# Two-layer encoder with mixture of experts: buffers placed ahead in 1 MB slots, and the latents' products behind the stick-breaking ones

## The chip, the cores and the metric

The kernel runs on one core of one Trainium2 chip. The metric is the time of one execution on the device, in microseconds (us); the time of a kernel is the median of its runs.

## The reference

Input x is 256 tokens by 1024 features, float32. Two layers, each with a mixer part and an expert part, then a last RMS norm. Cut to what matters:

```python
def hybrid_layer(x, ...):
    proj = rms_norm(x, norm1_g) @ w_in                   # 1024 -> 416 + 768 + 256
    ya = mla_mixer(proj[:, :256], proj[:, 256:384], proj[:, 384:416], ...)   # latents: 8 heads
    yb = stick_breaking_mixer(q, k, v)                   # 4 heads of 64, softplus and a reversed cumsum
    yc = pool_mixer(proj[..., o4:], pool_w, pool_scale)  # means over 2, 4, 8, 16 tokens
    x = x + concat(ya, yb, yc) @ w_out
    return x + hier_moe(rms_norm(x, norm2_g), ...)       # 4 groups x 8 experts of 256, top 2 of one group
def reference(x, ...):
    for l in range(2):
        x = hybrid_layer(x, ...)
    return rms_norm(x, final_g)
```

## The kernel before

All weights are float32 and are read once, in one ordered stream of tiles of 128 partitions by 16 KB (2 MB), each with one DMA from the queue of SP. The stream of a layer: the input projection in `a0` and `a1` (1.9 MB each), `v` (the columns of the stick-breaking values and of the pooling), `mid` (up-projections of the latents, pooling, router), `w0` and `w1` (output projection), 32 tiles `h00` to `h73` (gate and up weights of experts, 4 to each of 8 groups), and 16 tiles `d00` to `d33` (down weights: quarter of the features, pair of groups). The next layer's `a0`, `v`, `a1` stand among the `d` tiles, and `fg`, the gain of the last norm, behind `d13` of layer 1. `h22` is the third tile of group 2.

Memory for this stream and for large working buffers (`mHL`, the mixers' outputs in two parts; `wHL`, the split weights; `xHL`, the split input; `kq`, keys and queries; `tp`, transposed tokens and parts for the experts; `sHL`, stick-breaking weights in two parts) is given out by `Ring` (L49 to L115): 11 buffers of 2 MB (`pair`) and 3 of 1 MB (`one`), each taken from a list of free ones (`idle`) and given back as a whole. The program is built twice. The first build, the rehearsal, counts a tick at each take, get and drop of a buffer; `rehearsed` (L100) then gives each tile of the stream the first tick from which, up to its use, fewer than 11 pairs are taken. The second build issues the tile's DMA at this tick. It is a count only: which buffer a tile gets is decided by who is first in the list.

A layer in order of the program: `arrive` and `measure` transpose and square one quarter of the features at a time while the previous layer's expert quarters are added; `project_in(q, part)` (L343) multiplies quarter q with the input projection, parts 0 and 1 the 416 latent columns (12 products), parts 2 and 3 the 512 columns of the stick-breaking queries and keys (24 products). Every product of float32 weights is made of three, from a high and a low part of each operand, which DVE, ACT and POOL split off (`parts`, L224; `split` L256 goes 3 pieces ahead). In the last quarter each part has a step behind it: `scales` (L335, products of the inverse norms), `latents` (L382, square sums of the latents, and `dg`, the identity times the inverse norm), `rescale` (L398, latents times their norm), `heads` (L413, the product `ones` by `dg` that spreads the norms, and the scaled queries and keys).

`mixers` (L428) then does one value block, transposes the latents (L273), another value block, the stick-breaking scores (16 products, `zb`), and from there fills PE with what is left: in layer 0 six value blocks, then `keys(0)`, `keys(1)`, `latent_values`, four `latent_queries`; in layer 1, where six blocks of the values were done beside the experts, the keys, values and queries themselves. Between these stand the softplus pieces of ACT, for two heads each (Abs, Exp, Ln; L523 to L525), with a maximum and an addition on DVE (L530) and `stick_parts` (L504). Attention, the output projection and `route` follow; then `experts` (L836): `hidden(g)` takes 4 `h` tiles, `down` a half of a `d` tile. A buffer is given back when its last column is used. The program order of each engine is the order of the code; semaphores order the engines among one another.

Of the kernel before, what the change touches and what calls it, by code (L numbers as in the profile page):

```python
# [22 lines left out]
NPAIR, NONE = 11, 3  # L23
# [3 lines left out]
SM_UK, SM_UV, SM_PW, SM_RT = 2048, 2560, 3072, 3328  # L27
# [14 lines left out]
class Ring:  # L42
# [5 lines left out]

    def __init__(self, nc, pool, plan):  # L49
        self.nc, self.pool, self.plan = nc, pool, plan  # L50
        self.idle = {2: deque(range(NPAIR)), 1: deque(range(NONE))}
        self.stream, self.issued, self.now, self.cut = [], 0, 0, {}
        self.live, self.first, self.spans, self.kind = {}, {}, {}, {}

    def tile(self, dtype, n):
        i = self.idle[n].popleft()
        name = f"{('one', 'pair')[n - 1]}{i}"
        return n, i, self.pool.tile([128, 2048 * n], dtype, name=name, tag=name)

    def tick(self):  # L60
        self.now += 1
        while self.plan and self.issued < len(self.stream) and self.plan[self.issued] <= self.now:
            name, src, then = self.stream[self.issued]
            self.live[name] = self.tile(F32, 2)
            for a, b in self.cut.get(name, ((0, src.shape[1]),)):
                self.part(name, src, a, b)
            self.issued += 1
            for f in then:
                f()

    def part(self, name, src, a, b):

        self.nc.sync.dma_start(self.live[name][2][:src.shape[0], a:b], src[:, a:b])  # L73

    def take(self, name, dtype=F32, n=1):
        if self.plan:
            self.live[name] = self.tile(dtype, n)
        self.tick()
        self.first[name], self.kind[name] = self.now, n
        return self.live[name][2] if self.plan else self.pool  # L80
# [6 lines left out]
    def get(self, name):  # L87
        self.tick()
        self.first.setdefault(name, self.now)
        return self.live[name][2] if self.plan else self.pool  # L90

    def drop(self, *names):
        for n in names:
            if self.plan:
                size, i, _ = self.live.pop(n)
                self.idle[size].append(i)
            self.spans.setdefault(n, []).append((self.first.pop(n), self.now + 1))
        self.tick()

    def rehearsed(self):  # L100

        used = {n: np.zeros(self.now + 3, int) for n in (1, 2)}
        for name, v in self.spans.items():
            for a, b in v:
                used[self.kind.get(name, 2)][a:b] += 1
        assert used[1].max() <= NONE and used[2].max() <= NPAIR, (used[1].max(), used[2].max())
        plan, now, used = [], 1, used[2]
        for name, _, _ in self.stream:
            use = self.spans[name][0][0]
            full = np.flatnonzero(used[now:use] >= NPAIR)  # L110
            now = min(use, now + full[-1] + 1) if len(full) else now
            used[now:use] += 1
            plan.append(now)
        return plan
# [6 lines left out]
class Net:  # L121
    def __init__(self, tc, ctx, a, plan):
# [17 lines left out]
        def add(name, src, *then):  # L140
            r.stream.append((name, src, then))

        def w(l, *names, then=()):
            for n in names:
                add(f"{n}.{l}", a[n][l], *then)
# [3 lines left out]
        r.cut = {"a0.0": ((0, 928),), f"d33.{L - 1}": ((0, 2048), (2048, 3072), (3072, 4096))}  # L149
        rest = [lambda c=c: r.part(*r.stream[0][0:2], *c) for c in ((928, 1856), (1856, 3712))]  # L150
        w(0, "a0", then=[rest[0], load_x(1), rest[1], load_x(2), load_x(3)])
        w(0, "a1", then=[self.tables])
        w(0, "v")
        for l in range(L):
            w(l, "mid", "w0", "w1")
            for g in range(8):
                for i in range(4):
                    add(f"h{g}{i}.{l}", a["wh"][(l * 8 + g) * 4 + i])
            for q in range(4):
                for p in range(4):  # L160
                    add(f"d{q}{p}.{l}", a["wd"][(l * 4 + q) * 4 + p])
                if l + 1 < L:
                    w(l + 1, *(("a0", "v"), (), ("a1",), ())[q])
                elif q == 1:
                    add("fg", a["fg"])
# [67 lines left out]
    def weights(self, l):  # L233

        add = lambda name, c, n, last, how=0: self.feed.append((f"{name}.{l}", c, n, last, how))
        value = lambda k: add("v", k * 512, 512, k == 7)
        for q in range(4):
            for c, n in ((0, 416), (416, 512)):
                for k in (2 * q, 2 * q + 1):
                    add(f"a{k // 4}", k % 4 * 928 + c, n, c and k % 4 == 3, l + q == 0)  # L240
# [5 lines left out]
        add("mid", SM_UK, 512, False, 1)  # L246
        add("mid", SM_UV, 512, False, 1)
        for j in range(4):
            add("mid", j * 512, 512, False, 1)
        for c in (6, 7, 4, 5, 0, 1, 2, 3):  # L250
            for n in range(2):
                add(f"w{c < 4:d}", c % 4 * 1024 + n * 512, 512, n and c in (5, 3))
# [3 lines left out]
    def split(self, ahead=AHEAD):  # L256

        while self.feed and len(self.ready) <= ahead:
            name, c, n, last, how = self.feed.popleft()
            piece = self.ring.get(name)[:, c:c + n]  # L260
# [4 lines left out]
            if last:  # L265
                self.ring.drop(name)
# [68 lines left out]
    def scales(self):  # L335
# [5 lines left out]
        V.tensor_tensor(self.rr, self.rr, self.widths[:, None, :].to_broadcast([128, 2, 2]), op=OP.mult)  # L341

    def project_in(self, q, part):  # L343
# [3 lines left out]
        if part < 2:  # L347
# [6 lines left out]
        if q == 3:  # L354
# [765 lines left out]
```

## Time and profile before

| | us |
|---|---|
| runs | 631.49, 627.99, 627.11 |
| median | 627.99 |
| profiled execution | 630.48 |
| its span | 628.9 |
| PE busy | 539.5 (86% of the span) |
| DVE busy | 255.0 (41%) |
| ACT busy | 145.5 (23%) |
| POOL busy | 94.0 (15%) |
| stream of weights | 227.32 MB, 86.9% of the DMA engines' time |

The profile is of one execution. Busy time is a union of instructions; what matters for the end is where an engine is idle and what ended the idle time. 1.6 us of the profiled execution lie outside the span.

### The profile page before, as it was taken

How to read it: one execution, taken by the hardware profiler on the slowest of the kernel's cores; microseconds unless marked ns; L12 is line 12 of the kernel's file. 1: busy time of each engine (PE TensorE's matmuls, PEld its weight loads, DVE VectorE, ACT ScalarE, POOL GpSimd, SP SyncE). 2: the span in 40 equal slices, each digit the busy share in tenths (PEclk: the TensorE clock that was granted, in tenths of full speed). 3: DMA queues.
4: the chain of work that ended last, by engine and by line, in shares of the span. 5: the costliest groups of instructions: out<-in, count | busy, mean ns of one | idle time of the engine just before them, and what ended most of it. 6: DMA issues, size and time to landing. Idle time of an engine off the chain costs nothing. (4 is left out here: it accounts for less than half of the span.)

```text
span 628.9 us, 10437 instructions
## 1 busy us (share of the span) xinstructions
PE 539.5 (86%) x4296; PEld 360.4 (57%) x4296; DVE 255.0 (41%) x660; ACT 145.5 (23%) x359; POOL 94.0 (15%) x138
## 2 busy tenths in 40 slices
PE   8989999888888849699997899997888885849994
PEld 7959877454544415466666777753455551535662
DVE  4778665322232212423337776543322221111332
ACT  4466453100000011222224654410000001102221
POOL 2544222100000000111112232310000000000001
PEclk9999999989998888799999889999989988778998
DMA  8995667899999999999999156589999999999931
GB/s 319 417 422 244 267 269 287 350 399 426 428 426 430 423 425 425 428 429 422 431 427 425 68 209 271 214 348 430 428 428 426 426 428 426 424 427 426 425 153 68
DMA packets 18444, 228.69 MB, mean 364 GB/s; under 512 B 2129, under 2 KB 3409, under 8 KB 4690
## 3 DMA queue, kind: packets, MB, share of 16 engines
q1 hardware_dynamic: 17954, 227.32, 86.9%
q8 instruction: 37, 0.61, 0.4%
q10 hardware_dynamic: 432, 0.59, 0.3%
q14 instruction: 21, 0.17, 0.1%
HBM read 226.85 MB, written 1.05 MB: 362 GB/s over the span
## 5 line engine op out<-in xcount | busy, mean ns | idle before, releaser
L211 PE MATMUL ps<-pair,one 128*32 128x256 f32 (+2 forms) x2060 | 190.9, 502 | 19.9 <-PEq L966 13.4
L211 PE MATMUL ps<-pair,pair 128*128 128x512 f32 (+2 forms) x576 | 126.3, 365 | 4.0 <-POOL pair L229 2.3
L211 PEld LDWEIGHTS ps<-pair,one 128*32 128x32 f32 (+1 forms) x2060 | 62.4, 113 | 113.6 <-issue 87.8
L211 PEld LDWEIGHTS ps<-pair,pair 128*128 128x128 f32 x576 | 93.9, 192 | 28.7 <-issue 10.1
L211 PE MATMUL ps<-one,x 128*128 128x128 f32 x512 | 78.5, 317 | 29.1 <-DVE one L819 28.7
L211 PEld LDWEIGHTS ps<-one,x 128*128 128x128 f32 x512 | 72.1, 225 | 35.9 <-DVE one L819 35.7
L229 DVE TENSOR_TENSOR pair<-ps,pair 128x256 fp32r<-128x256 f32 (+1 forms) x74 | 31.9, 431 | 119.9 <-ACT pair L279 119.9
L229 POOL TENSOR_TENSOR pair<-pair,pair 128x512 fp32r<-128x512 f32 (+1 forms) x38 | 49.4, 1300 | 172.2 <-DVE pair L281 111.6
L279 ACT ACTIVATE pair<-ps 128x256 fp32r<-128x256 f32 (+2 forms) x80 | 33.1, 414 | 137.0 <-PE ps L211 136.6
L211 PE MATMUL ps<-pair 128*128 128x256 f32 (+1 forms) x320 | 61.3, 314 | 1.5 <-DVE low L560 0.6
L211 PEld LDWEIGHTS ps<-pair 128*128 128x128 f32 x320 | 46.0, 193 | 20.7 <-issue 15.8
L229 DVE TENSOR_TENSOR pair<-pair,pair 128x512 fp32r<-128x512 f32 (+1 forms) x54 | 46.6, 866 | 23.9 <-ACT pair L279 23.2
L868 ACT ACTIVATE one<-ps 128x256 f32<-128x256 f32 x16 | 6.1, 383 | 213.7 <-PE ps L211 213.7
L871 DVE TENSOR_REDUCE ws<-ps 128x1 f32<-128x256 f32 x16 | 6.8, 425 | 104.0 <-PE ps L273 104.0
L830 DVE TENSOR_TENSOR one<-ps,vec 128x512 f32<-128x512 f32 x32 | 22.1, 692 | 57.0 <-PE ps L211 56.8
L846 POOL TENSOR_TENSOR one<-one,comb 128x128 f32<-128x128 f32 x32 | 12.6, 399 | 192.3 <-DVE one L819 167.7
L279 ACT ACTIVATE pair<-pair 128x512 fp32r<-128x512 f32 (+1 forms) x54 | 32.7, 612 | 19.1 <-PE ps L211 9.3
L211 PE MATMUL ps<-ident,ones 128*128 128x128 f32 x172 | 28.7, 297 | 1.6 <-POOL ident L180 1.6
L273 PE MATMUL ps<-ident,one 128*128 128x128 f32 x128 | 23.3, 286 | 5.0 <-DVE pair L873 2.9
L273 PEld LDWEIGHTS ps<-ident,one 128*128 128x128 f32 x128 | 14.4, 141 | 22.3 <-issue 13.8
L211 PEld LDWEIGHTS ps<-ident,ones 128*128 128x128 f32 x172 | 24.2, 205 | 4.4 <-issue 2.8
L211 PE MATMUL ps<-one,pair 128*128 128x256 f32 x128 | 20.2, 314 | 4.5 <-DVE one L231 2.5
(138 smaller groups left out, 397.5 us busy)
## 6 DMA issues: line engine op xcount, KB each, us to landing
pair<-in_wh SPq DMA_DIRECT2D x64, 2048.0 KB, 18.8
pair<-in_wd SPq DMA_DIRECT2D x31, 2048.0 KB, 34.4
pair<-in_w SPq DMA_DIRECT2D x4, 2048.0 KB, 20.9
pair<-in_a SPq DMA_DIRECT2D x3, 1856.0 KB, 25.1
pair<-in_v SPq DMA_DIRECT2D x2, 2048.0 KB, 25.9
pair<-in_mid SPq DMA_DIRECT2D x2, 1808.0 KB, 20.6
x<-in_x SPq DMA_DIRECT2D x4, 256.0 KB, 5.8
pair<-in_wd SPq DMA_DIRECT2D x1, 1024.0 KB
```

The costliest lines, as they stand in the source:

```text
L211: self.nc.tensor.matmul(out, lhsT, rhs, start=start, stop=stop, skip_group_check=True)
L229: V.tensor_tensor(lo, in_, hi.bitcast(F32), op=OP.subtract)
L273: self.nc.tensor.transpose(out, in_, self.ident)
L279: nc.scalar.activation(out, in_, AF.Copy, scale=1.0 if scale is None else scale)
L830: self.nc.vector.tensor_tensor(xs[:, 4 * n:4 * n + 4], v3(self.ps[:, b0 + n], 4, 128), self.vec[:, l, 8 + 4 * n:12 + 4 * n, None].to_broad ...
L846: G.tensor_tensor(d4, d4, comb[:, t, 4 * g:4 * g + 4, None].to_broadcast([128, 4, 32]), op=OP.mult)
L868: A.activation(h, ps[:, 2, 0:256], AF.Silu)
L871: V.tensor_reduce(ws, ps[:, 3, 256:512], axis=AX.X, op=OP.add)
```

## The change

Memory stays 25 MB, now as 25 slots of 1 MB (`PAIRS = 12` pairs and a single one). All places are decided after the rehearsal: the working buffers first, each at a fixed place over its whole life, then the stream, tile after tile, in the places that are left. A tile has two halves (units) of 1 MB, which are got and dropped one by one. It is loaded with one DMA if a pair of slots is free, inside the experts ("calm") or if that is no later than the first half alone; otherwise with two DMAs, each half in a slot of its own. `a0` and `a1` are always loaded in halves. `fg` takes one slot. Column orders of `mid` and `w0` follow the halves. The core of `rehearsed`:

```diff
-        used = {n: np.zeros(self.now + 3, int) for n in (1, 2)}
...
-        plan, now, used = [], 1, used[2]
-        for name, _, _ in self.stream:
-            use = self.spans[name][0][0]
-            full = np.flatnonzero(used[now:use] >= NPAIR)
-            now = min(use, now + full[-1] + 1) if len(full) else now
...
+        for w in sorted(range(len(places)), key=lambda w: (-self.works[w][1], self.works[w][2] == F32, w)):
+            name, size, dtype, a, b = self.works[w]
...
+            busy[fit[0]:fit[0] + size, a:b] = True
...
+            first = alone(0, now)
+            if merge and len(units) == 2:
...
+                t, i = min((when((i, i + 1), now, ends), i) for i in range(0, n - 1, 2))
...
+                if t <= spans[0][0] and (t <= first[0] or calm[t]):
+                    plan.append((t, e, (0, 1), i))
```

In the last quarter the two products change places, with the steps behind them:

```diff
-            for c, n in ((0, 416), (416, 512)):
+            for c, n in ((416, 512), (0, 416)) if q == 3 else ((0, 416), (416, 512)):
...
-        if part < 2:
+        if (part < 2) != (q == 3):
...
-        if q == 3:
-            (self.scales, self.latents, self.rescale, self.heads)[part]()
+        if q == 3 and part != 2:
+            (self.scales, self.heads, None, self.latents)[part]()
```

`dg` is made in `scales`. `rescale` is called in `mixers`, all its evictions on DVE. There the scores `zb` come first, and one order serves both layers (`more(n)` does up to n value blocks, `soft(h, i)` is piece i of the softplus of heads h and h + 1):

```diff
+        soft(0, 0)
+        more()
+        soft(0, 1)
+        self.rescale()
+        soft(0, 2)
+        more()
+        soft(2, 0)
...
+        soft(0, 3)
+        self.parts(*ck, ps[:, 5, 0:256], vec[:, l, 18:19])
+        more(2)
+        soft(2, 1)
+        soft(2, 2)
         queries()
+        ring.drop("cw")
+        more(2)
+        soft(2, 3)
         ev("a", kv[64:128, 0::2], ps[64:128, 5, None, 256:512].to_broadcast([64, 4, 256]))
         ev("v", kv[0:64, 1::2], ps[0:64, 5, None, 256:512].to_broadcast([64, 4, 256]))
...
+        more(2)
+        ring.drop("xHL")
...
+        values_out()
+        stick_parts(0)
+        keys(0)
+        keys(1)
+        stick_parts(2)
+        latent_values()
```

On SP, in the mixers and the routing of layer 0, this is the order of the stream's transfers before: `h03`, `h10` to `h13`, `h20` to `h23`, each in a new buffer.

```order
L73 DMA pair_218<-in_wh 128x4096
L73 DMA pair_662<-in_wh 128x4096
L73 DMA pair_692<-in_wh 128x4096
L73 DMA pair_761<-in_wh 128x4096
L73 DMA pair_828<-in_wh 128x4096
L73 DMA pair_897<-in_wh 128x4096
L73 DMA pair_968<-in_wh 128x4096
L73 DMA pair_970<-in_wh 128x4096
L73 DMA pair_1081<-in_wh 128x4096
```

And now: `h03` (first row) to `h23` (last row), where `pair_116`, `pair_118` and `pair_120` are the places in which `h00`, `h01` and `h02` lie.

```order
L79 DMA pair_108<-in_wh 128x2048 x2
L79 DMA pair_110<-in_wh 128x2048 x2
L79 DMA pair_112<-in_wh 128x2048
L79 DMA pair_102<-in_wh 128x2048
L79 DMA pair_112<-in_wh 128x2048
L79 DMA pair_97<-in_wh 128x2048 x2
L79 DMA pair_114<-in_wh 128x2048
L79 DMA pair_102<-in_wh 128x2048
L79 DMA pair_114<-in_wh 128x2048
L79 DMA pair_964<-in_wh 128x4096
L79 DMA pair_116<-in_wh 128x4096
L79 DMA pair_118<-in_wh 128x4096
```

`h03` to `h20` now go out in halves, `h21` whole (`pair_964`), and `h22` goes into the place of `h00`, `h23` into that of `h01`.

On PE, from the last quarter of layer 1 on, before: the 12 latent products, the 24 of queries and keys, `ones`, a value block, the transposes, the other block, and the first scores.

```order
L211 MATMUL ps<-pair_2227,pair_2225 128x416 x12
L211 MATMUL ps<-pair_2225,pair_2227 128x256 x24
L211 MATMUL ps<-one_2226,ones 128x128 x2
L211 MATMUL ps<-pair_2227,pair_2225 128x512 x6
L273 MATMUL ps<-ident,one_2226 128x128 x8
L211 MATMUL ps<-pair_2227,pair_2225 128x512 x6
L211 MATMUL ps<-one_2900 128x256 x2
L211 MATMUL ps<-one_2900 128x128 x2
```

And now, from the 24 products to the keys (`one,pair_2177`, 256 columns):

```order
L280 MATMUL ps<-pair_2176,pair_2177 128x256 x24
L280 MATMUL ps<-pair_102,ones 128x128 x2
L280 MATMUL ps<-pair_2177,pair_2176 128x416 x12
L280 MATMUL ps<-one 128x256 x2
L280 MATMUL ps<-one 128x128 x2
L280 MATMUL ps<-one 128x256 x2
L280 MATMUL ps<-one 128x128 x2
L280 MATMUL ps<-pair_2177,pair_2176 128x512 x12
L343 MATMUL ps<-ident,pair_102 128x128 x8
L280 MATMUL ps<-one,pair_2177 128x256 x12
```

The latent products follow `ones`, the scores and both value blocks come before the transposes, and the keys right behind these.

On ACT at the same place before: the scaled norms, splits, the evictions of latent keys and queries (`ps,vec`), and the first Abs (L523) and Exp (L524) behind them.

```order
L421 ACTIVATE one_2900<-ps 128x256 x2
L279 ACTIVATE pair_2227<-pair_2559 128x512 x2
L279 ACTIVATE one_2939<-ps,vec 128x256 x3
L279 ACTIVATE pair_2940<-ps 64x4x256
L279 ACTIVATE one_2905<-ps,r_2816 128x512
L279 ACTIVATE pair_2227<-pair_2559 128x512
L279 ACTIVATE pair_2940<-ps 64x2x256
L523 ACTIVATE one_2938<-ps 128x768
L279 ACTIVATE pair_2940<-ps 64x2x256
L524 ACTIVATE one_2938<-one_2938 128x768
```

And now, from the first Abs (L529) on, with Exp (L531), Ln (L533) and the copy of `stick_parts` (L585):

```order
L529 ACTIVATE pair_108<-ps 128x768
L349 ACTIVATE pair_2177<-pair_118 128x512
L531 ACTIVATE pair_108<-pair_108 128x768
L533 ACTIVATE pair_108<-pair_108 128x768
L349 ACTIVATE pair_2177<-pair_118 128x512
L529 ACTIVATE pair_108<-ps 128x768
L349 ACTIVATE one<-ps,vec 128x256
L531 ACTIVATE pair_108<-pair_108 128x768
L533 ACTIVATE pair_108<-pair_108 128x768
L349 ACTIVATE one<-ps,vec 128x256 x2
L349 ACTIVATE pair_97<-ps 64x4x256
L349 ACTIVATE pair_102<-ps,r_2755 128x512
L585 ACTIVATE pair_141<-pair_108 128x768
```

The Exp and Ln of the second pair of heads now stand between the eviction of the latent keys and the two of the queries.

## Rows read from the trace of the kernel before

**Rows 1.** Page, part 2: GB/s in each of the 40 slices (15.7 us each).
```profile
GB/s 319 417 422 244 267 269 287 350 399 426 428 426 430 423 425 425 428 429 422 431 427 425 68 209 271 214 348 430 428 428 426 426 428 426 424 427 426 425 153 68
```

**Rows 2.** List of PE's waits: engine, line, releaser: us in total, times, longest.
```profile
PE ps L211 <- DMA pair<-in_fg: 7.9, 1, 7.9
...
PE ps L211 <- DMA pair<-in_wd: 5.3, 1, 5.3
...
PE ps L211 <- POOL pair L507: 0.6, 1, 0.6
```

**Rows 3.** Chain that ended last: start us, us, what.
```profile
537.29 26.28 DMA pair<-in_fg
```

**Rows 4.** Windows, core 0: busy of each engine, PEclk, DMA share, GB/s.
```profile
430.00:560.00 130.00, 103.14 (x872) 56.55 (x870) 31.81 (x80) 7.03 (x16) 4.75 (x12) 0.91 1.01 427
```

**Rows 5.** Timeline of SP's DMA issues: start us, us, line, out<-in, count.
```profile
102.76 0.80 SPq L73 DMA_DIRECT2D pair<-in_wh  x2
...
115.35 0.33 SPq L73 DMA_DIRECT2D pair<-in_wh  x1
...
132.48 0.33 SPq L73 DMA_DIRECT2D pair<-in_wh  x1
...
418.94 0.33 SPq L73 DMA_DIRECT2D pair<-in_wh  x1
...
434.45 0.33 SPq L73 DMA_DIRECT2D pair<-in_wh  x1
```

**Rows 6.** DMA issues at 65.1, 132.5, 434.4 us: KB each, us to landing.
```profile
pair<-in_wh SPq DMA_DIRECT2D x1, 2048.0 KB, 8.0
...
pair<-in_wh SPq DMA_DIRECT2D x1, 2048.0 KB, 13.4
...
pair<-in_wh SPq DMA_DIRECT2D x1, 2048.0 KB, 12.6
```

**Rows 7.** Timeline of PE, mixer of layer 0: start us, us, count, [idle before <-releaser].
```profile
30.88 0.61 PE L211 MATMUL ps<-one,ones 128*128 128x128 f32 x4
...
31.24 1.63 PE L211 MATMUL ps<-pair,pair 128*128 128x512 f32 x6
...
34.04 1.23 PE L273 MATMUL ps<-ident,one 128*128 128x128 f32 x8 [1.16 <-DVE one L408]
...
44.85 5.76 PE L211 MATMUL ps<-pair,pair 128*128 128x512 f32 x17 [1.57 <-POOL pair L229]
```

**Rows 8.** Timeline of PE, mixer of layer 1.
```profile
331.49 5.38 PE L211 MATMUL ps<-pair,pair 128*128 128x416 f32 x36 [0.56 <-ACT pair L279]
...
339.71 1.23 PE L273 MATMUL ps<-ident,one 128*128 128x128 f32 x8 [1.01 <-DVE one L408]
...
346.34 1.55 PE L211 MATMUL ps<-one,pair 128*128 128x256 f32 x6 [2.51 <-DVE one L231]
...
357.88 1.46 PE L211 MATMUL ps<-one,pair 128*128 128x256 f32 x10 [1.43 <-DVE pair L229]
```

**Rows 9.** Timelines of DVE and POOL at 26 to 31 us, of DVE at 331 to 338.
```profile
27.90 1.25 DVE L340 TENSOR_TENSOR rr<-r 128x4 f32<-128x4 f32 x1 [0.28 <-POOL r L307]
...
30.14 0.47 DVE L395 TENSOR_SCALAR one<-ident,r 128x128 f32<-128x128 f32 x2
...
27.84 1.29 POOL L229 TENSOR_TENSOR pair<-pair,pair 128x512 fp32r<-128x512 f32 x1
...
333.23 0.16 DVE L340 TENSOR_TENSOR rr<-r 128x4 f32<-128x4 f32 x1
```

**Rows 10.** Timeline of ACT, mixer of layer 1.
```profile
343.88 0.84 ACT L279 ACTIVATE one<-ps,vec 128x256 fp32r<-128x256 f32 x2 [2.57 <-PE ps L211]
...
350.29 0.83 ACT L524 ACTIVATE one<-one 128x768 f32<-128x768 f32 x1
```

**Rows 11.** Windows, two stretches behind waits of PE; columns as in rows 4.
```profile
46.10:49.50 3.40, 3.40 (x10) 2.61 (x8) 2.07 (x4) 2.83 (x4) 1.35 (x3) 0.50 1.00 424
...
346.50:349.90 3.40, 3.17 (x13) 2.87 (x14) 3.02 (x4) 2.79 (x6) 0.00 (x0) 0.50 0.57 243
```

More of the change, by code (lines that the diff above doesn't have):

```diff
@@ L50, in __init__ @@
         self.nc, self.pool, self.plan = nc, pool, plan
[L51 to L58, printed above, removed]
+        self.stream, self.now, self.cut, self.calm = [], 0, {}, []
@@ new lines, in __init__, with at, add @@
+        self.works, self.spans, self.live, self.hosts = [], {}, {}, {}
+        self.taken, self.issued = 0, 0
+    def at(self, slot, n, dtype):
+        i = slot // 2
+        if self.hosts.get(i, (None,))[0] != dtype:
+            name, size = (f"pair{i}", 4096) if i < PAIRS else ("one", 2048)
+            self.hosts[i] = dtype, self.pool.tile([128, size], dtype, name=name, tag=name)
+        c = slot % 2 * 2048
+        return self.hosts[i][1][:, c:c + 2048 * n]
+    def add(self, name, src, units=((0, 2048), (2048, 4096)), merge=True, then=()):
+        self.stream.append((name, src, units, merge, then))
@@ L60, in tick @@
     def tick(self):
         self.now += 1
[L62 to L66, printed above, removed]
-            self.issued += 1
[L68 to L73, printed above, removed]
+        while self.plan and self.issued < len(self.plan[1]) and self.plan[1][self.issued][0] <= self.now:
+            _, entry, us, slot = self.plan[1][self.issued]
+            self.issued += 1
+            name, src, units, _, then = self.stream[entry]
+            first, last = units[us[0]][0], units[us[-1]][1]
+            t = self.at(slot, len(us), F32)
+            for u in us:
+                self.live[name, u] = t[:, units[u][0] - first:units[u][1] - first]
+            for a, b in self.cut.get((name, us[-1]), ((0, last - first),)):
+                self.nc.sync.dma_start(t[:src.shape[0], a:b], src[:, first + a:first + b])
+            if us[-1] < len(then):
+                for f in then[us[-1]]:
+                    f()
@@ L114, in rehearsed @@
-        return plan
+        n, end = 2 * PAIRS + 1, self.now + 3
+        busy = np.zeros((n, end), bool)
+        kinds = np.zeros((n, end), int)
+        places = [None] * len(self.works)
+        for w in sorted(range(len(places)), key=lambda w: (-self.works[w][1], self.works[w][2] == F32, w)):
+            name, size, dtype, a, b = self.works[w]
+            kind = 1 + (dtype == F32R)
+            if size == 2:
+                fit = [i for i in range(0, n - 1, 2) if not busy[i:i + 2, a:b].any()]
+            else:
+                fit = [i for i in [n - 1, *sorted(range(n - 1), key=lambda i: (not busy[i ^ 1, a], i))]
+                       if not busy[i, a:b].any() and (i == n - 1 or kind == 1 and not (kinds[i ^ 1, a:b] == 2).any())]
+            assert fit, name
+            busy[fit[0]:fit[0] + size, a:b] = True
+            kinds[fit[0]:fit[0] + size, a:b] = kind
+            places[w] = fit[0]
@@ new lines, in when @@
+        def when(slots, now, ends):
+            t = now
+            for i, e in zip(slots, ends):
+                for j in ((i, i ^ 1) if i < n - 1 else (i,)):
+                    bad = np.flatnonzero(busy[j, now:e] if j == i else kinds[j, now:e] == 2)
+                    if len(bad):
+                        t = max(t, now + bad[-1] + 1)
+            return t
+        calm = np.zeros(end, bool)
+        state = 0
+        for begins, t in self.calm:
+            calm[t:] = begins
+        plan, now = [], 1
@@ L534, in mixers @@
[L534 to L547 removed]
+        more(2)
+        ring.drop("xHL")
+        sH, sL = (v3(t, 4, 384) for t in ring.two("sHL", F32R))
@@ L548, in mixers @@
+        values_out()
[4 more added lines that the diff above has]
+        latent_values()
+        for j in range(4):
+            latent_queries(j)
         ring.drop("cT")
```

201 lines of the change are left out of this document (102 added, 99 removed).

## The prediction

> **What bounds the kernel now.** I read the page's 40 slices first, then the list of PE's waits, the chain that ended last, and the timelines of the two stretches in which the weight stream stops. Weights come as one ordered stream of 2 MB tiles. The slices show two kinds of stretch [rows 1]: about 427 GB/s, and two holes, slices 4 to 8 (47 to 126 us, 244 to 350 GB/s) and slices 23 to 27 (346 to 424 us, down to 68 GB/s). The holes are the mixers and routing of layer 0 and layer 1: the buffers are full, and the stream moves only as one comes free. Behind each hole the stream runs without a gap (427 GB/s over 130 us [rows 4]) until PE, which eats faster, catches up with it: PE waits 5.3 us for a `d` tile of layer 0 and 7.9 us for `fg` in layer 1 [rows 2]. The chain that ended last goes back through that `fg` transfer [rows 3], and from there PE runs to the end without a wait for DMA. So the end is late by as much as the stream is late behind the hole of layer 1, and layer 1 starts late by as much as the stream is late behind the hole of layer 0 (that wait for a `d` tile). A saving on PE in a mixer counts since it makes the `h` tiles free sooner: the stream resumes when PE frees `h00`.
>
> **The change, part by part.**
> Placing ahead. The memory is the same, 25 MB; what changes is who may lie where. Bytes and the rate in full stretches stay, so I cost the loops over experts at nothing: there the planner still issues whole 2 MB tiles, one for each two halves freed. In the holes half tiles go out when one 1 MB slot is free, which lets `h10` to `h20` trickle in. I set this at nothing too: in both kernels `h21` and all before it are released by buffers of the mixer, the last at 102.76 us in layer 0 [rows 5], and a lone tile takes 8.0 us [rows 6] (4.9 back to back, 2.1 MB at 427 GB/s); so it has landed before the next slot comes free at 115.35, and what half a tile gains in time is lost in waiting for `h00`.
> The price is at `h22`. Today the planner counts buffers by number: when mHL and wHL are dropped, two pairs go to `h21` and `h22` at 102.76 us and right behind it [rows 5], since tp finds some other free pair later. With fixed places slots 0 and 1 stay kept for tp, and the built order shows `h22` in the place of `h00`, hence behind its release: 115.35 us in layer 0, 418.94 in layer 1, the times at which today `h23` goes out [rows 5]. The queue is empty by then, so the first of them takes 8.0 us [rows 6], each of the next five (`h23` to `h33`) 4.9.
> Layer 0: 115.35 + 8.0 + 5 x 4.9 = 147.9 us for `h33`, against 132.48 + 13.4 = 145.9 today [rows 5, 6]: 2.0 us later. (Today's own stream has a small gap there, which is why it isn't a whole tile of 4.9.)
> Layer 1: 418.94 + 8.0 + 24.5 = 451.4, against 434.45 + 12.6 = 447.1 [rows 5, 6]: 4.3 us later.
> If the release of other slots gave one tile more in time, both terms would be 0; if the gap of layer 0 came on top, the first would be 4.9: ends 0 and 9.2 for the two.
>
> Mixer of layer 0 (stick-breaking queries and keys first, then latents). New waits: the product that sums over partitions (`ones`) needs the scales, and it moves ahead of the 12 latent products, which take 2.4 us (12 of them with 416 columns and 24 of the heads with 256 take 5.38 us together in layer 1 [rows 8]; shared out by columns, 2.4 and 3.0). It would be due at 30.88 - 2.4 = 28.5, but rr ends at 29.15, and a second product on it (short like the 0.16 us at 333.23) and dg, 0.47 us, stand behind it [rows 9], to 29.8: 1.3 us of waiting. The transposes wait for the rescaled latents, as now. Today the last latent product ends at 30.88 - 3.0 = 27.9 and the transposes start at 34.04, 6.1 us later, of which PE waits 1.16 [rows 7]; in the new order 16 score products (1.5 us by their columns) and two value blocks (2 x 1.63 [rows 7]) lie between, 4.8 us, and all four evictions are on DVE: at least 1.3 us of wait, I take 1.5. Removed: 1.16 before the transposes and 1.57 before the value products [rows 7], with a smaller one of 0.3 behind it, as values no longer stand in one block of 36. 1.3 + 1.5 - 3.0 = -0.2. Ends: if each new wait costs half as much again and nothing is removed, +3; if the new waits vanish and the stretch at half clock that now follows the 1.57 us (3.4 us at a granted 0.50, 1.2 of 2.4 GHz [rows 11], worth 1.7) goes too, -4.7.
>
> Mixer of layer 1 (two value blocks only, so little to fill with). Removed: 1.01 before the transposes, 2.51 before the first keys, 1.43 before the last latent queries [rows 8], and 0.6 for a POOL part of the stick-breaking weights [rows 2]: 5.6 us. Added: before `ones` 0.6 (rr here takes 0.16 us at 333.23 [rows 9]), before the transposes 1.0 (latent products end at 331.49 + 2.4 = 333.9, transposes start at 339.71: 5.8 us of chain, less 4.8 of cover), before the second keys 0.7 (as long as one of ACT's pieces there [rows 10]), and the largest, before the first keys. Keys need both parts of the latent keys and the queries' evictions, which free the bank that keys write. Today the wait is 2.51 us behind evictions that start at 343.88 [rows 8, 10]: 346.34 - 343.88 = 2.46. In the new order ACT has Exp and Ln of the second pair of heads between them, 0.83 us each [rows 10], and the eviction of the latent keys (0.42) ahead: 2.46 + 1.66 + 0.42 = 4.5, less 0.3 for the last transposes, which run during the first of these: 4.2 us. Nothing fills it, as PE has only transposes ahead and keys behind. Sum 0.6 + 1.0 + 0.7 + 4.2 - 5.6 = +0.9. Today a half-clock stretch follows the 2.51 (3.4 us [rows 11]) and another like it stands behind the 1.43; I let one of the two go, -1.7, as the 4.2 us will bring one of its own: -0.8. Ends: +2.7 (both stay, one small wait more), and -5.1 (keys wait as today, 2.5, instead of 4.2, no new stretch, and the two new small ones gone).
>
> Behind these waits stand all of PE's products of the mixer, and the `h00` release behind them; nobody else waits in a way that sets the end. Loads at the start are cut in the same pieces, and the tail after `fg` runs off PE alone: nothing.
>
> Sum: 2.0 - 0.2 + 4.3 - 0.8 = +5.3 us against the profiled execution: 630.48 + 5.3 = 635.8. That execution is 2.5 us above the median of the runs, 627.99, so 633.3 for a median.
>
> One rule is weighed. The row: rr, a DVE product of 4 numbers, takes 1.25 us beside a POOL split that starts 0.06 us before it, and 0.16 us where no split runs [rows 9]. The Trainium skill, SBUF — State Buffer, section "SBUF: two separate sides", says that DVE with two operands in SBUF and GpSimd take one pair of ports as an exclusive lock, so the loser waits out the whole instruction; the row agrees. By it, the moved rr of layer 1 can fall beside a split as well, and the wait before `ones` would be 0.6 + 1.1 = 1.7; by the row of today it is 0.6.
>
> **Rivals.**
> A, slower: the reordered mixers don't pay. On PE the wait before the keys is 4.2 us or more in layer 1, with ACT's Exp and Ln ahead of the evictions, and the waits taken away come back elsewhere; +3 and +2.7 in place of -0.2 and -0.8: 2.0 + 3 + 4.3 + 2.7 = +12, 640. It decides once the two mixers together lose anything: then the sum passes 6.3. For it: ACT and DVE run one chain there, today already 2.51 us late [rows 8]. Against it: four waits really disappear. Chance 0.20. The port rule alone is its smaller form: 5.3 + 1.1 = 6.4, 634.4, chance 0.05.
> B, faster: half tiles free so much sooner that the stream doesn't fall behind and PE no longer waits on it: 5.3 + 7.9 = 13.2 us off [rows 2], 614.8. For it: in slice 23 only 68 GB/s are moved [rows 1], so there is room. Against: the order shows `h22` behind `h00`, and a buffer must be free before any transfer, however small. Chance 0.10.
> C, faster by little: stream as forecast, +6.3, but the mixers give -4.7 and -5.1: -3.5, 624.5. For it: half clock and waits both go. Against: the 4.2 us. Chance 0.12.
> The change may also not do what it says of the stream: a late `h22` hidden because PE isn't at its tail. Against this stand the waits for `d` and `fg` [rows 2], which pass lateness on in full; with the mixers' -1.0 alone it would give 627, and I leave it 0.03.
>
> **How the numbers follow.** Forecast 0.50, with its own range from 627 (streams' terms 0 to 2 lower, mixers 4 better) to 638. The measurement tells about 1% of this kernel, 6.3 us, from no change: borders 621.7 and 634.3. Faster: B 0.10 and 0.03 of C: 0.13. Slower: A 0.20, the port 0.03 and 0.17 of the forecast: 0.40. Same: the rest, 0.47. The range from 621 to 641 leaves out B, the bottom of C and the top of A.
>
> **What would show it.** Right: in the changed profile `h22` goes out right behind the release of `h00` in both layers, `h33` lands 2 and 4 us later counted from that release, waits for `in_wd` and `in_fg` stay or grow, PE waits about 4 us before the first keys of layer 1, and no wait stands before the values of layer 0. Wrong: `h22` out before `h00` is used, the GB/s of slices 23 to 27 clearly above today's with less waiting for `fg`, or PE reaching the first `h` product of layer 1 more than 4 us sooner after the start of the last quarter than now.

## The result, and the profile after

| | before | changed |
|---|---|---|
| median of the runs, us | 628.79 | 635.81 |
| lowest to highest | 627.11 to 631.49 | 634.51 to 636.98 |
| profiled execution | 630.48 | 636.98 |

The changed kernel takes 1.0107 times as long (95% interval 1.0064 to 1.0151), 7.0 us more by the medians and 6.5 by the profiled executions. The page's GB/s in 40 slices (15.9 us each) shows the two holes again. That of layer 0 is deeper than in [rows 1] (174 in the fifth slice, 267 before); in layer 1 the five slices from the 23rd on sum to less (173 + 117 + 302 + 275 + 221 = 1088, before 1110):

```profile
GB/s 319 418 425 292 174 254 301 250 433 427 425 426 428 424 427 422 428 425 428 428 416 404 173 117 302 275 221 430 427 428 428 427 429 427 424 426 427 425 173 67
```

In the list of PE's waits, DMA now stands for 24.4 us (before: 13.2 by the two rows of [rows 2], 14.4 with a wait of 1.2 for `in_wh`). The wait of 4.1 us before the first keys and the two before the transposes (2.9 together, 2.2 in the kernel before) are the reordered mixers':

```profile
PE ps L280 <- DMA pair<-in_wh: 10.7, 4, 2.9
...
PE ps L280 <- DMA pair<-in_wd: 7.5, 1, 7.5
...
PE ps L280 <- DMA pair<-in_fg: 6.2, 1, 6.2
...
PE ps L280 <- DVE one L300: 4.1, 1, 4.1
...
PE ps L343 <- DVE pair L478: 2.9, 2, 1.9
```

The chain that ended last goes through `fg` as in [rows 3], 7 us later, and from there PE runs to the end in 55.8 us:

```profile
544.94 25.63 DMA pair<-in_fg
...
570.71 55.83 PE ps L280 x576
```

SP's timeline, the issues of `h22` and `h33` in layer 0 and in layer 1. As forecast, `h22` goes out behind the release of `h00`:

```profile
116.21 0.33 SPq L79 DMA_DIRECT2D pair<-in_wh  x1
...
133.88 0.33 SPq L79 DMA_DIRECT2D pair<-in_wh  x1
...
421.09 0.33 SPq L79 DMA_DIRECT2D pair<-in_wh  x1
...
437.40 0.33 SPq L79 DMA_DIRECT2D pair<-in_wh  x1
```

And how long each took to land (KB each, us). A transfer into the empty queue took 8.9 and 8.8 us, and `h33` landed at 133.88 + 15.8 = 149.7 and 437.40 + 17.0 = 454.4, where [rows 5, 6] give 145.9 and 447.1 for the kernel before:

```profile
pair<-in_wh SPq DMA_DIRECT2D x1, 2048.0 KB, 8.9
...
pair<-in_wh SPq DMA_DIRECT2D x1, 2048.0 KB, 15.8
...
pair<-in_wh SPq DMA_DIRECT2D x1, 2048.0 KB, 8.8
...
pair<-in_wh SPq DMA_DIRECT2D x1, 2048.0 KB, 17.0
```

PE's timeline in the mixer of layer 0 (`ones`, the transposes, the last value blocks, the latent queries), against [rows 7]:

```profile
28.71 0.71 PE L280 MATMUL ps<-pair,ones 128*128 128x128 f32 x4 [1.02 <-DVE pair L414]
...
38.07 1.85 PE L343 MATMUL ps<-ident,pair 128*128 128x128 f32 x8 [1.93 <-DVE pair L478]
...
48.54 1.43 PE L280 MATMUL ps<-pair,pair 128*128 128x512 f32 x5 [0.62 <-POOL pair L298]
...
54.06 6.01 PE L280 MATMUL ps<-one,pair 128*128 128x256 f32 x48 [1.28 <-DVE pair L351]
```

Of the waits before the values (1.57 and a smaller one of 0.29) 0.62 is left; waits of 1.02 and 1.28 are new, and that before the transposes has grown from 1.16 to 1.93. In layer 1 (`ones`, transposes, both keys), against [rows 8], the first keys wait 4.08 us and `ones` not at all:

```profile
339.21 0.61 PE L280 MATMUL ps<-pair,ones 128*128 128x128 f32 x4
...
347.47 1.28 PE L343 MATMUL ps<-ident,pair 128*128 128x128 f32 x8 [0.94 <-DVE pair L478]
...
352.84 1.65 PE L280 MATMUL ps<-one,pair 128*128 128x256 f32 x6 [4.08 <-DVE one L300]
...
354.89 1.65 PE L280 MATMUL ps<-one,pair 128*128 128x256 f32 x6 [0.40 <-DVE pair L351]
```

Windows of two stretches at half clock (granted 0.50), one from the transposes of layer 0 on, one at the end of the keys' wait of layer 1. Before, there was one of 3.4 us in the mixer of layer 0 (46.1) and two of 3.4 us in that of layer 1 (346.5 [rows 11] and 367.0):

```profile
38.40:41.80 3.40, 3.40 (x13) 2.78 (x11) 2.43 (x6) 0.48 (x1) 1.14 (x3) 0.50 1.01 429
...
352.40:359.20 6.80, 5.96 (x20) 5.09 (x21) 6.74 (x9) 5.71 (x10) 3.86 (x4) 0.50 0.27 114
```

### The profile page after: what moved, and what is told of

It reads as the page before. It is cut to its first block, busy times and chain, and to the rows that moved or that the text cites. A ratio compares the mean times of both kernels' runs of the same rounds, so it can differ in the third digit from the quotient of the medians.

```text
span 635.4 us, 10511 instructions
## 1 busy us (share of the span) xinstructions
PE 537.0 (85%) x4296; PEld 357.3 (56%) x4296; DVE 254.3 (40%) x664; ACT 144.9 (23%) x355; POOL 94.2 (15%) x138
## 5 line engine op out<-in xcount | busy, mean ns | idle before, releaser
L280 PE MATMUL ps<-pair,pair 128*32 128x512 f32 (+4 forms) x1624 | 245.8, 516 | 12.7 <-DMA pair<-in_wh 10.7
L280 PEld LDWEIGHTS ps<-pair,pair 128*32 128x32 f32 (+2 forms) x1624 | 128.7, 140 | 108.6 <-issue 80.8
L280 PE MATMUL ps<-pair,x 128*128 128x128 f32 x512 | 74.0, 304 | 29.2 <-DVE pair L894 27.4
L280 PE MATMUL ps<-pair,one 128*32 128x256 f32 (+1 forms) x1036 | 77.9, 410 | 20.8 <-PEq L1040 13.3
L280 PEld LDWEIGHTS ps<-pair,x 128*128 128x128 f32 x512 | 67.6, 213 | 35.9 <-DVE pair L894 35.8
L349 ACT ACTIVATE pair<-ps 128x256 fp32r<-128x256 f32 (+4 forms) x82 | 34.3, 420 | 140.1 <-PE ps L280 139.8
L280 PE MATMUL ps<-pair 128*128 128x256 f32 (+3 forms) x336 | 61.8, 312 | 0.0
L280 PEld LDWEIGHTS ps<-pair 128*128 128x128 f32 (+1 forms) x336 | 46.8, 188 | 19.2 <-issue 16.2
L280 PEld LDWEIGHTS ps<-pair,one 128*32 128x32 f32 (+1 forms) x1036 | 31.2, 116 | 44.3 <-issue 18.7
L280 PE MATMUL ps<-one,pair 128*128 128x256 f32 (+2 forms) x184 | 24.0, 314 | 5.8 <-DVE one L300 4.1
## 6 DMA issues: line engine op xcount, KB each, us to landing
pair<-in_wd SPq DMA_DIRECT2D x31, 2048.0 KB, 33.4
```

What stands on the lines that cost most here:

```text
L280: self.nc.tensor.matmul(out, lhsT, rhs, start=start, stop=stop, skip_group_check=True)
L349: nc.scalar.activation(out, in_, AF.Copy, scale=1.0 if scale is None else scale)
```

## The experiments

All edits are to the changed kernel unless said otherwise. Each ratio is to the kernel before on the same chip.

| kernel | median | ratio (95% interval) |
|---|---|---|
| changed | 635.81 | 1.0107 (1.0064, 1.0151) |
| e1_tp | 629.43 | 1.0013 (0.9986, 1.0040) |
| e2_oldmix | 635.95 | 1.0109 (1.0055, 1.0162) |
| e4_keys | 638.11 | 1.0147 (1.0095, 1.0200) |
| e5_a0 | 637.92 | 1.0142 (1.0102, 1.0182) |
| e6_mixbylayer | 626.24 | 0.9941 (0.9919, 0.9963) |
| e7_all | 625.81 | 0.9940 (0.9920, 0.9960) |
| e8_oldmix_tp | 627.45 | 0.9963 (0.9941, 0.9984) |
| e9_keys | 626.04 | 0.9949 (0.9924, 0.9974) |
| e10_hold | 631.00 | 1.0021 (1.0005, 1.0037) |
| e11_taken | 637.17 | 1.0095 (1.0060, 1.0130) |
| e12_va | 626.88 | 0.9938 (0.9911, 0.9964) |

From each profiled execution, in us: the issue that waits for the release of `h00`, the landing of `h33` and of `d10`, the first product of the last quarter of layer 1. Where the trace has no landing of `d10` (before, e10_hold, e11_taken), it is the start of PE's first product on it less 0.05, as in the changed kernel.

| kernel | h00, layer 0 | h33 | d10 | last quarter | h00, layer 1 | h33 |
|---|---|---|---|---|---|---|
| before | 115.35 | 145.84 | 257.89 | 331.49 | 418.94 | 447.10 |
| changed | 116.21 | 149.65 | 263.19 | 335.83 | 421.09 | 454.36 |
| e1_tp | 115.78 | 144.36 | 257.87 | 330.51 | 415.71 | 444.03 |
| e2_oldmix | 111.85 | 145.27 | 258.81 | 331.82 | 418.29 | 452.00 |
| e4_keys | 115.35 | 148.68 | 262.21 | 335.02 | 419.59 | 452.63 |
| e5_a0 | 114.93 | 148.36 | 261.84 | 334.70 | 420.09 | 452.96 |
| e6_mixbylayer | 113.74 | 142.35 | 255.75 | 328.38 | 413.63 | 442.00 |
| e7_all | 112.50 | 142.56 | 255.41 | 328.88 | 413.17 | 442.10 |
| e8_oldmix_tp | 112.39 | 140.97 | 254.34 | 327.24 | 413.73 | 444.53 |
| e9_keys | 113.28 | 141.91 | 255.10 | 327.92 | 412.48 | 442.00 |
| e10_hold | 114.05 | 144.30 | 256.32 | 329.91 | 416.57 | 444.91 |
| e11_taken | 113.93 | 147.46 | 259.56 | 333.60 | 420.27 | 453.35 |
| e12_va | 114.50 | 143.08 | 256.48 | 329.53 | 413.26 | 442.55 |

**e1_tp: the place of tp.**

```diff
-                fit = [i for i in range(0, n - 1, 2) if not busy[i:i + 2, a:b].any()]
+                fit = [i for i in (range(0, n - 1, 2), (10,))[name == "tp"] if not busy[i:i + 2, a:b].any()]
```

> The changed kernel, with tp placed where h03 lies until then instead of in slots 0 and 1; h22 then goes out when mHL and wHL are dropped, as in the kernel before. Theory (the place kept for tp makes the stream late by 2.9 us in layer 0 and 5.1 in layer 1, counted from the release of h00 to the landing of h33): h22 goes out near 104 and 409 us, h33 lands 3 us earlier in layer 0 than in the changed kernel's trace (149.6) and some 8 earlier in layer 1 (454.4), the waits for d and fg shrink, and the time is 635.8 - 7 = 629, at least 4 us under the changed kernel. Rival (the new order of the mixers is what costs, the stream is hidden): h22 early as well, but the time stays within 2 us of 635.8.

Slots 10 and 11 are the place that `h03` of layer 0 has left by then. `h21` and `h22` go out together at 103.2 us, and `h23` takes the place of `h00` (timeline of SP, with layer 1's `h23`):

```profile
103.20 1.49 SPq L79 DMA_DIRECT2D pair<-in_wh  x2
...
115.78 0.33 SPq L79 DMA_DIRECT2D pair<-in_wh  x1
...
415.71 0.33 SPq L79 DMA_DIRECT2D pair<-in_wh  x1
```

From the release to `h33`: 28.6 and 28.3 us, against 33.4 and 33.3 in the changed kernel. PE's waits for DMA fall to 17.4 us:

```profile
PE ps L280 <- DMA pair<-in_fg: 7.7, 1, 7.7
...
PE ps L280 <- DMA pair<-in_wd: 7.2, 1, 7.2
...
PE ps L280 <- DMA pair<-in_wh: 2.5, 1, 2.5
```

The time falls by 0.9%, to that of the kernel before: the theory holds. The edit does a little more than its name says: with slots 0 and 1 free the plan puts other tiles elsewhere too, and 22 half tiles of `h` go out instead of 28.

**e2_oldmix and e8_oldmix_tp: the old order in the mixers**, without and with the free place for tp (`weights`, `scales`, `project_in`, `latents`, `rescale` and the first part of `mixers` as before).

```diff
-            for c, n in ((416, 512), (0, 416)) if q == 3 else ((0, 416), (416, 512)):
+            for c, n in ((0, 416), (416, 512)):
...
-        if q == 3 and part != 2:
-            (self.scales, self.heads, None, self.latents)[part]()
+        if q == 3:
+            (self.scales, self.latents, self.rescale, self.heads)[part]()
```

> The changed kernel with its 25 slots, but the last quarter and the mixers in the order of the kernel before (latents first, values and keys in their old places). Theory (the stream's place costs, the new order costs 0.9 us on PE in layer 0 and gives back 2.2 in layer 1): the waits of 4.1 us before the first keys and 1.9 before the transposes go, those of 2.5 and 1.2 come back, and the time is 635.8 + 1.3 = 637, within 3 us of the changed kernel. Rival (the new order of the mixers costs): 629 to 631. Rival (the order was worth more than 4 us): over 640.

> Both layers with the mixers in the order of the kernel before, and the place of tp as in e1_tp: the 25 slots alone, without the place that is held. Theory (the held place costs 6 to 8 us whatever the mixers' order): 636.0 - 7 = 629, and less than that by up to 1 since the first order is quicker in layer 0; against e6_mixbylayer 1 to 2 us slower. Rival (in the old order h22 was covered and the place of tp is worth less than 3 us): 633 to 636.

As long as tp's place is held, the order makes no difference that can be measured (1.0109 and 1.0107); freeing the place is worth 1.5% with the old order (e2 to e8) and 0.9% with the new (changed to e1). In layer 0 the old order releases `h00` at 111.9 to 112.4, without a stretch at half clock. Its waits there, PE's timeline of e2_oldmix (transposes, values, latent queries):

```profile
32.96 1.23 PE L343 MATMUL ps<-ident,one 128*128 128x128 f32 x8 [1.33 <-DVE one L478]
...
42.17 4.17 PE L280 MATMUL ps<-pair,pair 128*128 128x512 f32 x17 [0.57 <-POOL pair L298]
...
49.64 6.02 PE L280 MATMUL ps<-one,pair 128*128 128x256 f32 x48 [0.35 <-DVE pair L351]
```

1.33 + 0.57 + 0.35 = 2.3 us, where the new order waits 1.02 + 1.93 + 0.62 (values) + 1.28 = 4.9. So the new order costs 2.6 us there. In layer 1, from the start of the last quarter to the release of `h00`, it takes 85.2 to 85.4 us (changed, e1, e5, e6), the old order 86.5 (e2, e8): 1.2 us gained. That is rough to about 1 us: e7_all, with the program of e6_mixbylayer there, takes 84.3; its 6.8 us at half clock begin in the keys' wait, with PE busy for 3.27 us of them and not for 5.95 (windows of e6_mixbylayer, then of e7_all):

```profile
344.90:351.70 6.80, 5.95 (x20) 5.08 (x21) 6.74 (x9) 5.71 (x10) 3.85 (x4) 0.50 0.19 82
...
342.70:349.50 6.80, 3.27 (x13) 2.98 (x14) 4.83 (x8) 5.41 (x9) 2.70 (x4) 0.50 0.48 200
```

**e3_a0 and e5_a0: a0 and a1 whole.** e3_a0 asks for one transfer but gives the first half's slot back while the second half still has 192 columns in it, so that the next tile overwrites weights of a0 and a1; PE waited 17.0 us at one place behind DVE where no other kernel waits over 0.9, and its 655.8 us (1.0412) say nothing here. e5_a0 holds both slots until the last column.

```diff
-                    r.add(f"{n}.{l}", a[n][l], ((0, 1856), (1856, 3712)), False, then)
+                    r.add(f"{n}.{l}", a[n][l], ((0, 1856), (1856, 3712)), l > 0, then)
...
-                ends = [s[1] for s in spans]
+                ends = [s[1] for s in spans] if units[0][1] == 2048 else [spans[1][1]] * 2
```

> The changed kernel with a0 and a1 of layer 1 in one transfer each, as in the kernel before. In the changed kernel's trace the two halves of a0 take 5.9 us to land one behind the other where the whole took 4.4, and everything behind them is 1.5 us later. Theory (the halves cost that): the first tile of layer 0's d10 lands 1.5 us earlier counted from the landing of h33, PE waits 1.5 us less for it, and the time is 634.3. Rival (the order in which halves land differs, but the sum of bytes sets the time): d10 lands as far behind h33 as now, 113.5 us, and the time stays at 635.8 within 0.5.

> The changed kernel with a0 and a1 of layer 1 in one transfer each, both of whose slots are held until its last column is used. Theory (two transfers of half the size make the stream late): from the landing of h33 to that of d10 in layer 0 112.1 us pass instead of 113.5, PE waits 1.4 us less for d10, and the time is 635.8 - 1.4 = 634.4. Rival (it is the bytes that count): 113.5 us, and 635.8.

From `h33` to `d10` 113.5 us passed, as in the changed kernel, and the whole a0 took 5.8 us to land behind `d03` (246.25 to 252.04). PE's wait for `d10`:

```profile
PE ps L280 <- DMA pair<-in_wd: 7.3, 1, 7.3
```

The rival holds: the 1.4 us are not due to halves. In the three kernels with the old buffers (before, e10, e11) 112.0 to 112.1 us pass, in those with slots 112.9 to 113.5. Why is open; a tile somewhere between `d03` and `d13` takes 0.6 to 1.5 us too long in all traces but that of e1_tp, in the kernel before `d12`, behind `d10`, in the changed one a0, ahead of it.

**e4_keys and e9_keys: the queries' evictions first** (layer 1; e9_keys on top of e6_mixbylayer).

```diff
-        soft(2, 1)
-        soft(2, 2)
+        if not l:
+            soft(2, 1)
+            soft(2, 2)
         queries()
...
+        if l:
+            for i in (1, 2, 3):
+                soft(2, i)
```

> The changed kernel with, in layer 1 alone, the queries' evictions before the Exp and Ln of the second pair of heads. Theory (the 4.1 us before the first keys are ACT's Exp and Ln, 1.7 us, ahead of these evictions): the wait falls to 2.4 us, h00 of layer 1 is released 1 to 2 us sooner, and the time falls by as much, to 634 to 635. Rival (the wait is the chain from the transposes through DVE, which the order on ACT doesn't shorten): the wait stays over 3.5 us and the time at 635.8. Rival (what is saved there comes back at stick_parts and the latent queries): wait 2.4 us, time 635.8.

> e6_mixbylayer with the queries' evictions of layer 1 ahead of Exp and Ln of the second pair of heads, as in e4_keys. There the wait before the first keys fell from 4.1 to 2.5 us but waits of 0.8 and 1.5 us grew behind it, and from the start of the last quarter to the release of h00 84.6 us passed in place of 85.2. Theory (what is saved before the keys comes back behind them): 0 to 1 us under e6_mixbylayer, not to be told from it, 625 to 626. Rival (the keys' wait is worth its size): 1.6 us or more under it, 624.5 or less.

PE's timeline of e4_keys (first and second keys, latent queries):

```profile
350.48 0.98 PE L280 MATMUL ps<-one,pair 128*128 128x256 f32 x6 [2.52 <-DVE one L300]
...
352.25 1.65 PE L280 MATMUL ps<-one,pair 128*128 128x256 f32 x6 [0.80 <-DVE pair L351]
...
357.38 6.02 PE L280 MATMUL ps<-one,pair 128*128 128x256 f32 x48 [1.45 <-DVE pair L351]
```

The first wait fell by 1.56 us, as worked out from ACT's Exp and Ln (1.66), but 0.40 became 0.80 and 1.45 is new, so that the waits add up to 0.3 us more. What was saved came back behind the keys, as the second rival said. The traces are 0.7 us shorter all the same (84.6 for 85.3, in both), but they have 3.4 us at half clock there (from 351.8 and 344.7 on), the changed kernel and e6_mixbylayer 6.8. In the time nothing is left.

**e6_mixbylayer and e7_all: a version faster than both kernels.** Layer 0 in the old order, layer 1 in the new, tp's place free; e7_all also with a0 and a1 whole.

```diff
-            for c, n in ((416, 512), (0, 416)) if q == 3 else ((0, 416), (416, 512)):
+            for c, n in ((416, 512), (0, 416)) if q == 3 and l else ((0, 416), (416, 512)):
...
-        if (part < 2) != (q == 3):
+        if (part < 2) != (q == 3 and self.late):
```

> The place of tp as in e1_tp, layer 0 with its last quarter and mixers in the order of the kernel before, layer 1 in the new order. Theory (in the trace of e2_oldmix h00 of layer 0 is released at 111.9 us, in those of the new order at 115.4 to 116.2: the new order costs 4 us in layer 0 and saves 1.2 in layer 1 against the old): h00 of layer 0 released near 112 us, all behind it 4 us earlier than in e1_tp, 629.4 - 4 = 625.5. Rival (the 4 us come from the place of buffers or from that execution): 629, with the release at 115.

> e6_mixbylayer with a0 and a1 of layer 1 in one transfer each as well. Theory: 1.4 us less than e6_mixbylayer, near 624, clearly faster than both kernels; PE's wait for d10 in layer 0 shrinks from 7.2 us (e1_tp) to about 6. Rival (the halves don't matter): equal to e6_mixbylayer.

Both are 0.6% faster than the kernel before. e6_mixbylayer differs from e1_tp in layer 0 alone: 0.7% in the ratios, 2.0 us at the release of `h00`. The whole a0 adds nothing, as in e5_a0.

**e10_hold and e11_taken: the suspected cost put into the kernel before.** First as a count in the planner, then as a buffer:

```diff
 e10_hold
+        for (_, a), (b, _) in zip(self.spans["sHL"], self.spans["tp"]):
+            used[2][a:b] += 1
 e11_taken
         ring.drop("sHL")
+        self.tp = ring.two("tp", F32R)
...
-                hT, dTs = v3(ring.take("th"), 8, 256), ring.two("tp", F32R)
+                hT, dTs = v3(ring.take("th"), 8, 256), self.tp
```

> The kernel before with one number in its planner changed: a pair counts as taken from the drop of sHL to the take of tp, as the fixed place of tp does in the changed kernel. Nothing else: whole 2 MB tiles, the old mixers, the old buffers. Theory (the held place alone makes the stream late): h22 goes out behind the release of h00, h33 lands 115.4 + 8.8 + 5 x 4.9 = 148.7 us in layer 0, 2.8 later than in the kernel before, and 5.1 later in layer 1; the time is 628.8 + 7.9 = 636.7, between 634.5 and 638.5. Rival (half tiles or the fixed places make it late): at most 1.5 us over the kernel before.

> The kernel before with one line moved: the pair for tp is taken where sHL is dropped, and so lies empty until the experts use it, as the fixed place does in the changed kernel. (In e10_hold the planner only counted a pair less; that moves a transfer's place in the program, but the buffer handed out was the one long free, and h22 still went out at 101.84 us.) Theory (a buffer that is really held makes the stream late): h22 goes out behind the release of h00, h33 lands 2.0 to 2.9 us later in layer 0 and 4.3 to 5.1 later in layer 1, counted from that release, and the time is 630 + 6.3 to 8 = 636 to 638. Rival (half tiles or other parts of the new plan make it late): within 1.5 us of the kernel before.

e10_hold came out as its rival said, at 1.0021, but that doesn't speak for the rival: the edit did not hold a buffer. SP's timeline shows two transfers together at 101.46, `h22` the second:

```profile
101.46 0.80 SPq L73 DMA_DIRECT2D pair<-in_wh  x2
```

The planner's tick only puts the transfer at a place in the program; SP runs ahead of PE and waits for the buffer that it is given. The pair of sHL, meant to lie empty, went to `h10` from the list of free ones, and `h22` got that of wHL, both as in the kernel before. With the pair really taken, `h22` (first row; the second is `h33` of layer 1) goes out behind the release of `h00`:

```profile
113.93 0.33 SPq L73 DMA_DIRECT2D pair<-in_wh  x1
...
437.40 0.33 SPq L73 DMA_DIRECT2D pair<-in_wh  x1
```

`h33` lands after these (issues at 129.4 and 437.4, us in the last column):

```profile
pair<-in_wh SPq DMA_DIRECT2D x1, 2048.0 KB, 18.0
...
pair<-in_wh SPq DMA_DIRECT2D x1, 2048.0 KB, 16.0
```

That is 33.5 and 33.1 us behind the release of `h00`, 3.0 and 4.9 more than in the kernel before, and PE's waits for DMA are 23.9 us, close to the changed kernel's 24.4:

```profile
PE ps L211 <- DMA pair<-in_wh: 11.1, 5, 2.9
...
PE ps L211 <- DMA pair<-in_fg: 7.1, 1, 7.1
...
PE ps L211 <- DMA pair<-in_wd: 5.7, 1, 5.7
```

1.0095: nearly the whole difference of the change (1.0107), in a kernel without slots, half tiles or a new order. One reserve: of the 3.0 us in layer 0 1.5 lie between the landings of `h31` (136.20) and `h33` (147.46), 11.3 us for two tiles with the queue full, and for these no cause is shown; in layer 1 there is no such gap.

**e12_va: rescaling on DVE and ACT**, on top of e1_tp.

```diff
-                self.ev("v", self.cn[:, t, c], p[:, t, c], s2[:, t, j:j + 1])
+                self.ev("va"[t], self.cn[:, t, c], p[:, t, c], s2[:, t, j:j + 1])
```

> e1_tp with the latents' rescaling shared between DVE and ACT as in the kernel before, where it is all on DVE in the changed kernel. Theory (the four evictions in a row on DVE are why the transposes wait 1.93 us in layer 0): that wait falls to 1.2 to 1.5 us, the latent queries' wait of 1.28 stays, and the scan of layer 0 starts near 60. Rival (the wait is the chain of square sums, POOL's power and ACT's Exp): 1.9 us as now or more, since ACT has its softplus pieces ahead of the evictions.

PE's timeline of e12_va (transposes and latent queries of layer 0, transposes of layer 1):

```profile
37.85 1.22 PE L343 MATMUL ps<-ident,pair 128*128 128x128 f32 x8 [1.40 <-DVE pair L478]
...
52.31 6.01 PE L280 MATMUL ps<-one,pair 128*128 128x256 f32 x48 [1.28 <-DVE pair L351]
...
340.55 1.23 PE L343 MATMUL ps<-ident,pair 128*128 128x128 f32 x8 [0.33 <-DVE pair L478]
```

The waits before the transposes fell by 0.5 and 0.6 us, as the theory said. The ratio, 0.9938, lies 0.7% under that of e1_tp; the profiled executions are 0.8 us apart (627.65 and 626.88), so how much of the 0.7% is this edit stays open. Part of what the profiles differ by is the clock: e1_tp has 3.4 us at half clock in the mixer of layer 0 (from 39.8 on), e12_va none.

## Why the prediction was right or wrong

The time was forecast at 633.3 (621 to 641) and is 635.8; the difference between the profiled executions was forecast at +5.3 and is +6.5. The ratio, 1.07% slower, lies just over the border of 1% between "same" (0.47) and "slower" (0.40), and its interval reaches to either side.

Followed through the two profiled executions (changed less before): release of `h00` in layer 0 +0.9, `h33` +3.8, `d10` +5.3, last quarter of layer 1 +4.3, release of `h00` there +2.2, `h33` +7.3, `fg` +7.0, end +6.5. Against the terms of the sum:

- The held place: forecast 2.0 + 4.3, measured 33.44 - 30.49 = 2.95 and 33.27 - 28.16 = 5.1. The mechanism is shown from both sides: freeing the place takes 0.9 to 1.5% away (e1, e8), holding a buffer in the kernel before adds 0.95% (e11). The size was off by 0.8 to 1.0 in each layer, as the first transfer into the empty queue took 8.9 and 8.8 us and not the 8.0 of [rows 6].
- That lateness passes to the end in full: nearly right. PE waits 7.5 us for `d10` and 6.2 for `fg`; of 5.3 us at `d10` 4.3 reach the last quarter of layer 1, of 7.3 at `h33` there 6.5 reach the end. The wait for `fg` was to stay or grow and fell from 7.9.
- The mixer of layer 0, forecast -0.2: +0.9 at the release. Two things lie under it. The new order costs 2.6 us by its waits (at the release 2.9, e4 and e5 against e2, e7 and e8, all without a half-clock stretch there; 2.5 with one of 3.4 us on both sides, changed and e1 against e6 and e9). And the slots alone gain 1.7: at full clock the old order releases `h00` at 111.9 to 112.5 in slots (e2, e7, e8), at 113.9 to 114.1 in the old buffers (e10, e11). The step of this term that failed is "Removed: ... 1.57 before the value products": with the old order in slots that wait is 0.55 to 0.57 (e2, e7, e8), in the old buffers 1.56 to 1.57 (e10, e11; row of e10_hold below), so 1.0 of it goes with the slots. The order gains nothing there (0.62 with the new one). Why the slots shorten it is not shown. The sentence "Loads at the start are cut in the same pieces" is wrong as well, since `a1` of layer 0 now comes in halves; `ones` of the old order starts at 29.6 to 30.3 in slots, at 30.3 to 30.9 in the old buffers, and that the halves do this is likely, not shown.

```profile
44.40 4.19 PE L213 MATMUL ps<-pair,pair 128*128 128x512 f32 x17 [1.57 <-POOL pair L231]
```

- The waits themselves were near: `ones` 1.3 forecast and 1.02 measured, transposes 1.5 and 1.93, in layer 1 `ones` 0.6 and none, transposes 1.0 and 0.94, first keys 4.2 and 4.08, second keys 0.7 and 0.40. Missed were 1.28 before the latent queries of layer 0 and the 0.62 that is left before its values.
- The mixer of layer 1, forecast -0.8: from the last quarter's start to the release 85.3 us for 87.5, -2.2. About 1.2 of it is the order (e2, e8 against changed, e1, e5, e6). The waits agree: the forecast's own come to -0.1 and not +0.9, and three that it left alone (0.23, 0.37 and 0.62 us) went too. The half-clock term, -1.7, did not come: 6.8 us stood there before, 3.4 of them from 367.0 on and so not behind the wait of 1.43 (357.88), and 6.8 stand there now. Of the other 1.0, 0.8 lies between executions of the old order and buffers: e10 and e11 take 86.7 us. In e11 one half-clock stretch (349.8) stands in place of two, in e10 a wait of 0.85 in place of 0.37 and 1.43; that this is the reason is not shown.
- Not in the sum: 1.5 us between `h33` and `d10` (open), and 1.0 us gained from there to the last quarter of layer 1 (open as well).

That the sum came within 1.2 us is partly luck. The mechanism that carries it, the held place, is right and was put 1.8 us too low; the mixers together, forecast at -1.0, are -1.3, but by the order alone they lose (2.6 less 1.2), and what the slots gain in layer 0 hides it.

Of the rivals, B (half tiles free the stream) is refuted: with the same slots the time turns on one place. A's condition, mixers that together lose, is true of the order by itself (+2.6 - 1.2, and e1 is 0.5% slower than e8); in the changed kernel it is outweighed by the gain of the slots in layer 0 and by the 1.0 us of layer 1 that isn't the order's. On the pair of ports that DVE and GpSimd share as an exclusive lock (the Trainium skill, SBUF — State Buffer, section "SBUF: two separate sides"), the trace agrees: in layer 0 rr takes 1.03 us beside a POOL split that ends with it, and in layer 1 it was `dg`, beside such a split, that took 1.33 us instead of 0.47, while rr took 0.15:

```profile
27.18 1.07 POOL L298 TENSOR_TENSOR pair<-pair,pair 128x416 fp32r<-128x416 f32 x1
...
27.23 1.03 DVE L410 TENSOR_TENSOR rr<-r 128x4 f32<-128x4 f32 x1 [0.33 <-POOL r L377]
...
337.75 1.09 POOL L298 TENSOR_TENSOR pair<-pair,pair 128x416 fp32r<-128x416 f32 x1 [1.46 <-DVE rr L410]
...
337.79 1.33 DVE L414 TENSOR_SCALAR pair<-ident,r 128x128 f32<-128x128 f32 x2
```

It cost nothing there, since PE reached `ones` at 339.21, just behind the end of `dg` (339.12).

## What to carry to other kernels

A buffer placed ahead and kept empty until its use is taken from whatever streams through the rest: where the stream stops and starts again, one tile less ahead cost 3 to 5 us at each restart. Place such a buffer where a tile of the stream ends just before, and read from the order which release each transfer waits for; a planner's count of ticks doesn't tell it. Where one change does two things, try them apart by layer or by part: here the same reordering lost in one layer, gained in the other, and hid that the slots alone gain.

## What the runs showed of the hardware that was not expected

A 2 MB transfer into an empty queue took from 7.5 us (e11_taken, 68.30 to 75.83) to 9.2 (`h22` of e2_oldmix in layer 1, 418.29 to 427.54), and 8.9 in `h22` of the changed kernel, against 4.9 behind another; the 8.0 of the forecast is one such value. And the stretches at half clock differ from one profiled execution to another where instructions and waits are the same: the changed kernel has one of 3.4 us in the mixer of layer 0 (38.4), e4_keys and e5_a0, with the same program and the same waits there, have none, and release `h00` 0.9 and 1.3 us earlier.
